# Value columns of all heads projected in the first head, element products in the ring of the level tiles, and a group's value products issued behind its last masked copy

## The chip, the core and the metric

The kernel runs on one core of one Trainium2 chip. A core has a matrix engine (TensorE, PE in the profile; its weight loads are listed as PEld), a vector engine (VectorE, DVE), a scalar engine (ScalarE, ACT), GpSimd (POOL) and an engine that mostly issues transfers (SyncE, SP). Each engine works through its own queue in order and waits on semaphores for the others. Data lies in SBUF (128 partitions); TensorE writes to PSUM, which has eight banks of 512 float32 columns for each partition. The metric is the device time of one launch in microseconds (us); the median of several runs is compared.

## What is computed

One decoder layer for 2048 positions of width 1024. The part that matters here is the mixing stage: a normalised input is projected to queries, forget gates, values and output gates of four HGRN2 heads, and to queries, keys and values of a sliding-window attention with eight query heads, two key heads and a sink logit in the softmax.

```python
u = rmsnorm(h, norm_mix_w[l])
proj = u @ w_in[l]
hq, hf, hi, hg, att = jnp.split(proj, [...], axis=-1)
f = lb + (1.0 - lb) * jax.nn.sigmoid(hf)
o_hg = hgrn2_chunkwise(q_hg, k_hg, v_hg, log_f)     # v_hg is hi, 4 heads of 128 columns
o_hg = rmsnorm(o_hg, hg_norm_w[l]) * silu(hg)
o_att = sliding_window_attention_with_sinks(aq, ak, av, sinks[l])
h = h + jnp.concatenate([o_hg, o_att], axis=-1) @ w_out[l]
```

The recurrence of a head is `S_t = diag(f_t) S_{t-1} + k_t v_t^T`, `o_t = S_t^T q_t`, with `k_t = 1 - f_t`. After the mixing stage come a gated feed-forward stage with a short convolution and a final normalisation.

## The kernel before

The sequence is worked in two halves of 1024 positions (`HALF`). In each, the mixing stage runs over four heads `h`; with each head goes one pair of attention query heads `j = h`. Then come the output projection (`out_proj`), the feed-forward stage (`gate_up`, `down`), and in the tail of `down` the first units of the next half.

A dense product in float32 is made of three matmuls on parts: weights and input are each split into a rounded part (`hi`, `xh`) and a rest (`lo`, `xl`), and hi·xh, hi·xl and lo·xh are summed in PSUM. `prep` loads 1024 columns of weights (SP issues the load into a ring of three, tag `raw`), ACT makes the rounded copy (L192) and DVE the rest (L193). Both go to a ring of two (tags `hi` and `lo`), or, with `slots`, to the ring of eight tiles with tag `m` in the pool `hp`, which also holds input tiles, the heads' queries and attention outputs. `unit` (L214) then makes 48 matmuls of 512 columns for 128 output rows.

For one head, `hgrn` is a generator that is driven in pieces:

- the units `f` and `hq` and their evictions;
- the levels: first two element products of the two halves of the columns, then seven levels with block sizes 1 to 64. `summed_products` multiplies on DVE (L546), splits the product (ACT L547, DVE L548) and sums it over the partitions with two matmuls (L550, L551, tile `pdiag`); it is called twice for the diagonal and once for the first level. For each of the other levels ACT copies a rearranged part of `QK` into a tile `G` (L598), four matmuls make `plev` (L609; L604 at block size 32), and DVE multiplies `QK` in place (L612) for the next level. Tile `QK` and tile `f` have one buffer each;
- transposes of K (L646), state updates (L653 on TensorE, L657 on DVE);
- the gate unit `g`, the output products (L671, L672), a norm and a transpose (L687).

`attend` makes the unit `q`, then scores and softmax for two groups of four query blocks, and then, for each group: four transposes for each key head (L497, tile `ppt`), and two masked copies of each on DVE (L500, tiles `po` and `pp`: the block's own keys and those of the block before). From these, 16 value products (L508, tile `poT`, 64 output rows each; float32, two instructions each on TensorE) sum the two key blocks for four query blocks and two key heads. ACT copies the result out (L512; in the last pair L518, whose result the output projection reads).

Values of the recurrent heads come from `project_v`, called in heads 0 and 2, each time for two heads: eight tiles of 128 positions, each with 24 matmuls of 256 columns (L706 to L708, tile `pvv`), evicted by two scaled copies on ACT (L710). Its matmuls stand behind the levels in the program, and TensorE works on them while the levels' small matmuls wait for ACT and DVE. In heads 1 and 3 no projection stands there; head 3 has its gate unit ahead of the levels and the first units of the output projection (L214, tile `pop`) behind them.

The program's order is not the queues' order. A planner simulates the engines and puts instructions into each queue by program order and by when it expects their inputs; `tc.issue_after(x)` keeps what is traced inside it behind `x` on the same engine, without a semaphore. The buffers of a tag are given out as they come free, and a tile whose ring is full makes its first writer wait.

Of the kernel before, what the change touches and what calls it, by code (L numbers as in the profile page):

```python
# [8 lines left out]
F32 = mybir.dt.float32  # L9
F32R = mybir.dt.float32r  # L10
U32 = mybir.dt.uint32
I32 = mybir.dt.int32
AF = mybir.ActivationFunctionType
# [26 lines left out]
NEG = -1.0e30  # L40
UT = 7
RAW = 3
VB = 2
GB = 2
WARM = 12
TAIL_WARM = 7
LV = 4
# [3 lines left out]
def hymba_layer(ctx: ExitStack, tc: tile.TileContext, a: dict, out: bass.AP):  # L51
# [380 lines left out]
    def attend(hf, j, X, invb, KS, V, mix, p):  # L432

        o = unit(a["w_att"][j], X, "q")
        qT = slot(f"att{j}")
        for b, bs in halves():
            nc.vector.scalar_tensor_tensor(qT[:, bs], o[b], 0.125, invb[:, bs], op0=ALU.mult, op1=ALU.mult)
            nc.scalar.activation(qT[:, bs], qT[:, bs], AF.Identity, bias=C.bq[:, j:j + 1])
        yield
        scs = []  # L440
        for g in range(NB):
            sc = p.tile([P, 2, 4, P], F32, tag="sc", name="sc", bufs=2)
            gs = slice(g * 512, (g + 1) * 512)
            for kv in range(2):
                r, other = rows(kv), rows(1 - kv)

                qh, ql = [p.tile([P, 512], F32R, tag="pp", name=n, bufs=4) for n in ("qh", "ql")]
                nc.scalar.copy(qh[r], qT[r, gs])
                nc.scalar.copy(qh[other], qT[r, gs])
                nc.vector.tensor_tensor(ql[r], qT[r, gs], qh[r].bitcast(F32), op=ALU.subtract)  # L450
                nc.scalar.copy(ql[other], ql[r].bitcast(F32))
                for i0 in (0, 2):
                    pb = ps("at", "psc")
                    first = hf == 0 and g == 0 and i0 == 0
                    for i in range(2):
                        n = g * 4 + i0 + i
                        w0 = 1 if first and i == 0 else 0
                        o = pb[:, i * 256 + w0 * P:(i + 1) * 256]
                        ks = slice((n + w0) * P, (n + 2) * P)
                        for t, qx in enumerate((qh, ql)):  # L460
                            nc.tensor.matmul(o, qx[:, (i0 + i) * P:(i0 + i + 1) * P], KS[:, kv, ks],
                                             start=t == 0, stop=t == 1)
                    pv = pb.rearrange("p (i w k) -> p i w k", i=2, w=2)
                    dst = sc[:, kv, i0:i0 + 2]
                    if first:
                        nc.vector.memset(dst[:, 0], NEG)
                        nc.scalar.copy(dst[:, 1], pv[:, 1, 0])
                    else:
                        nc.scalar.copy(dst, pv[:, :, 0])
                    nc.vector.copy_predicated(  # L470
                        dst, C.own.bitcast(U32).unsqueeze(1).to_broadcast([P, 2, P]), pv[:, :, 1])
            m = p.tile([P, 2, 4], F32, tag="mx", name="m", bufs=2)
            nc.vector.tensor_reduce(m.rearrange("p a b -> p (a b)"),
                                    sc.rearrange("p a b c -> p (a b) c"), axis=AX.X, op=ALU.max)
            sk = C.sinkb[:, j].unsqueeze(2).to_broadcast([P, 2, 4])
            nc.vector.tensor_tensor(m, m, sk, op=ALU.max)
            es = p.tile([P, 2, 4], F32, tag="es", name="es", bufs=2)
            nc.vector.tensor_tensor(es, sk, m, op=ALU.subtract)
            nc.vector.tensor_scalar(m, m, -1.0, None, op0=ALU.mult)
            den = p.tile([P, 2, 4], F32, tag="den", name="den", bufs=2)  # L480
            for kv in range(2):
                for i in range(4):
                    nc.scalar.activation(sc[:, kv, i], sc[:, kv, i], AF.Exp, bias=m[:, kv, i:i + 1],
                                         accum_out=den[:, kv, i:i + 1])
            nc.scalar.activation(es, es, AF.Exp)
            nc.vector.tensor_tensor(den, den, es, op=ALU.add)
            nc.vector.reciprocal(den, den)
            nc.vector.tensor_tensor(sc, sc, den.unsqueeze(3).to_broadcast([P, 2, 4, P]), op=ALU.mult)
            scs.append(sc)
        yield  # L490
        for g, sc in enumerate(scs):
            pm = []
            for kv in range(2):
                pm.append([p.tile([P, 4, P], F32, tag="pp", name=n, bufs=4) for n in ("po", "pp")])
                pt = ps("at", "ppt")
                for i in range(4):
                    nc.tensor.transpose(pt[:, i * P:(i + 1) * P], sc[:, kv, i], ident)  # L497
                ptv = pt.rearrange("p (i q) -> p i q", i=4)
                for dst, mk in zip(pm[kv], (C.ownT, C.prevT)):
                    nc.vector.tensor_tensor(dst, ptv, mk.unsqueeze(1).to_broadcast([P, 4, P]), op=ALU.mult)  # L500
            oT = ps("at", "poT")
            for i in range(4):
                n = g * 4 + i
                noprev = hf == 0 and n == 0
                for prev in range(1 if noprev else 2):
                    for kv in range(2):
                        r = rows(kv)
                        nc.tensor.matmul(oT[r, i * P:(i + 1) * P], V[:, n + 1 - prev, r], pm[kv][prev][:, i],  # L508
                                         start=prev == 0, stop=noprev or prev == 1)
            gs = slice(g * 512, (g + 1) * 512)  # L510
            if j < ATT_J - 1:
                nc.scalar.copy(qT[:, gs], oT)  # L512
                mix[4 + j] = qT
            else:
                if g == 0:
                    mix[4 + j] = new_x()
                h, l = mix[4 + j]
                nc.scalar.copy(h[:, gs], oT)  # L518
                nc.vector.tensor_tensor(l[:, gs], oT, h[:, gs].bitcast(F32), op=ALU.subtract)
            yield  # L520

    def hgrn(hf, h, X, invb, vs, WG, mix, p, fu=None):
# [18 lines left out]
        ST = p.tile([P, TT, P], F32, tag="t4", name="ST", bufs=2)  # L541
        def summed_products(x, y):

            d = p.tile([P, 512], F32, tag="dd", name="dd", bufs=2)
            hi, lo = [p.tile([P, 512], F32R, tag="dg", name=n, bufs=4) for n in ("dh", "dl")]
            nc.vector.tensor_tensor(d, x, y, op=ALU.mult)  # L546
            nc.scalar.copy(hi, d)  # L547
            nc.vector.tensor_tensor(lo, d, hi.bitcast(F32), op=ALU.subtract)  # L548
            o = ps("hg", "pdiag")
            nc.tensor.matmul(o, ones_r, hi, start=True, stop=False)  # L550
            marks[1] = nc.tensor.matmul(o, ones_r, lo, start=False, stop=True)  # L551
            return o
# [142 lines left out]

    def project_v(hf, parts, X, rs, p):

        v = [p.tile([P, TT, P], F32, tag="v", name="v", bufs=VB) for _ in range(2)]
        for tt in range(TT):
            o = ps("mm", "pvv")  # L700
            t = slice(tt * P, (tt + 1) * P)
            for kt in range(KT):
                hi, lo = parts[kt // 4]
                xh, xl = X[kt]
                c = slice((kt % 4) * 256, (kt % 4 + 1) * 256)
                nc.tensor.matmul(o[:, 0:256], xh[:, t], hi[:, c], start=kt == 0, stop=False)  # L706
                nc.tensor.matmul(o[:, 0:256], xl[:, t], hi[:, c], start=False, stop=False)
                nc.tensor.matmul(o[:, 0:256], xh[:, t], lo[:, c], start=False, stop=kt == KT - 1)  # L708
            for i in range(2):
                nc.scalar.activation(v[i][:, tt], o[:, i * P:(i + 1) * P], AF.Identity, scale=rs[:, tt:tt + 1])  # L710
        return v

    def split_into(h, l, src, eng=None):
        return (nc.scalar.copy(h, src),  # L714
# [480 lines left out]
    for hf in range(NH):  # L1195
        X, kv, invb, rs, f0 = nxt
        with ExitStack() as st:
# [5 lines left out]
            for h in range(HG):  # L1203
# [4 lines left out]
                if h == HG - 1:  # L1208
                    next(at)
                    next(hg)  # L1210
                    for kt in (0, 4, 1, 5, 2, 6):
                        M[kt] = split(mix[kt])
                    next(hg)
                elif h % 2 == 0:
                    next(at)
                    wv = [prep(a["w_v"][h // 2, s]) for s in range(2)]
                    next(hg)
                    vs += project_v(hf, wv, X, rs, p)
                else:
                    next(hg)  # L1220
                    next(at)
# [21 lines left out]
def _layout(i):  # L1243
# [14 lines left out]
    rows = [ar(P) + h * P for h in range(4)]  # L1258
    rows += [512 + np.concatenate([j * HD + ar(HD), (j + 4) * HD + ar(HD)]) for j in range(4)]
    w_out = i["w_out"][0][np.concatenate(rows)]  # L1260
    w_v = np.stack([cols(w_in, 1024 + pr * 256 + ar(256)).reshape(P, 2, D).transpose(1, 0, 2) for pr in range(2)])
    conv = np.concatenate([i["conv_w"][0], i["conv_b"]], 0)
    d = {
        "xT": x.T.reshape(KT, P, S),
# [37 lines left out]
```

## Time and profile before

| what | value |
|---|---|
| median of three runs | 2175.64 us |
| lowest and highest | 2173.93 and 2177.19 us |
| the profiled execution's own time | 2174.83 us |
| its span, first to last instruction | 2173.1 us |
| granted TensorE clock | 0.999 |
| moved by DMA | 258.09 MB, mean 119 GB/s |

The profile is one execution. Busy shares and durations are those of single instructions; matmuls overlap, so their distance in time, not their duration, is what they cost. Rows of groups give the line, the engine, the operation, the tiles (output, then inputs), the shape and the count, then the busy time, the mean duration in nanoseconds, and the idle time of that engine just before them with what ended it. Rows of the timeline give the start and the duration in us. Rows of windows give a stretch, its length, and the busy time of TensorE, weight loads, DVE, ACT and POOL in it, each with its number of instructions, then the granted clock, the DMA share and GB/s.

### The profile page before, as it was taken

The numbers are of one execution on the slowest core, as the hardware profiler recorded it, in microseconds if no ns is written. First come the engines' busy times: TensorE is split into PE (matmuls) and PEld (weight loads), VectorE is DVE, ScalarE is ACT, GpSimd is POOL, SyncE is SP. The second block draws the span as 40 slices with busy tenths as digits, with TensorE's granted clock in tenths as the row PEclk, the third lists the DMA queues.
The fourth block names the chain that finished last, engine by engine and source line by source line (L and its number), as shares of the span: only waits on it lengthen the run. The fifth ranks groups of instructions, "written<-read, shape, count | busy, mean of one in ns | idle before, by whom it ended". The sixth has DMA issues, their size and how long they took to land.

```text
span 2173.1 us, 29038 instructions
## 1 busy us (share of the span) xinstructions
PE 2151.3 (99%) x11136; PEld 1809.6 (83%) x11136; DVE 1659.9 (76%) x2446; ACT 1094.1 (50%) x1902; POOL 6.0 (0%) x28
## 2 busy tenths in 40 slices
PE   9999999999999999999999999999999999999998
PEld 7988987888888888788889889878888888888888
DVE  6677677688887878785866776777978888887766
ACT  6556556564444445335736466555544443444353
POOL 1000000000000000000000000000000000000000
PEclk9999999999999999999999999999999999999999
DMA  4101112413232235964631111124133323259643
GB/s 156 49 30 39 49 40 78 136 59 127 92 126 89 96 117 167 375 223 163 205 127 39 42 37 49 47 70 147 58 116 102 117 82 126 93 190 396 226 142 131
DMA packets 94387, 258.09 MB, mean 119 GB/s; under 512 B 11416, under 2 KB 17576, under 8 KB 94248
## 3 DMA queue, kind: packets, MB, share of 16 engines
q1 hardware_dynamic: 88992, 251.30, 34.2%
q10 hardware_dynamic: 5256, 4.94, 0.8%
q8 instruction: 87, 1.43, 0.3%
q14 instruction: 52, 0.43, 0.1%
HBM read 195.10 MB, written 57.15 MB: 116 GB/s over the span
## 4 chain that ended last, share of the span: by engine, by line
PE 93%; DVE 3%; ACT 2%; DMA 1%; issue 1%; SPq 0%; ACTq 0%; DVEq 0%
PE X L885 7%; PE pop L214 7%; PE X L887 7%; PE X L886 7%; PE hq L214 4%; PE f L214 4%; PE q L214 4%; PE g L214 4%; PE Y L885 4%; PE Y L886 4%; PE Y L887 4%; PE pdx L1098 3%; PE pdx L1096 3%; PE pdx L1097 3%; PE pdy L1096 3%; PE pdy L1097 3%
## 5 line engine op out<-in xcount | busy, mean ns | idle before, releaser
L714 ACT CAST whi<-raw 128x1024 fp32r<-128x1024 f32 x88 | 92.6, 1052 | 109.1 <-PE X L886 68.2
L885 PE MATMUL X<-T,whi 128*128 128x512 f32 x352 | 136.9, 389 | 0.0
L886 PE MATMUL X<-T,whi 128*128 128x512 f32 x352 | 136.9, 389 | 0.0
L887 PE MATMUL X<-T,wlo 128*128 128x512 f32 x352 | 136.9, 389 | 0.0
L980 DVE SCALAR_TENSOR_TENSOR y<-ga,cw,y 128x1024 f32<-128x1024 f32 x88 | 112.4, 1280 | 26.0 <-ACT y L978 26.0
L892 ACT COPY u<-X 128x512 f32<-128x512 f32 x88 | 51.5, 585 | 133.2 <-PE X L887 133.0
L715 DVE TENSOR_TENSOR wlo<-raw,whi 128x1024 fp32r<-128x1024 f32 x88 | 107.2, 1219 | 0.0
L715 DVE TENSOR_TENSOR xld<-raw,xhd 128x1024 fp32r<-128x1024 f32 x72 | 80.9, 1132 | 21.7 <-ACT xhd L714 21.2
L192 ACT CAST whi<-raw 128x1024 fp32r<-128x1024 f32 x57 | 59.9, 1050 | 72.2 <-PE pop L214 28.6
L714 ACT CAST xhd<-raw 128x1024 fp32r<-128x1024 f32 x72 | 69.6, 977 | 47.3 <-DMA raw<-act1T 15.5
L193 DVE TENSOR_TENSOR wlo<-raw,whi 128x1024 fp32r<-128x1024 f32 x57 | 69.2, 1217 | 26.4 <-ACT whi L192 26.3
L214 PE MATMUL pop<-XH,wlo 128*128 128x512 f32 x256 | 85.9, 390 | 0.0
L214 PE MATMUL pop<-XL,whi 128*128 128x512 f32 x256 | 85.2, 390 | 0.0
L214 PE MATMUL pop<-XH,whi 128*128 128x512 f32 x256 | 85.0, 393 | 0.0
L886 PEld LDWEIGHTS X<-T,whi 128*128 128x128 f32 x352 | 66.1, 188 | 13.8
L885 PEld LDWEIGHTS X<-T,whi 128*128 128x128 f32 x352 | 66.1, 188 | 13.7
L887 PEld LDWEIGHTS X<-T,wlo 128*128 128x128 f32 x352 | 66.1, 188 | 13.7
L1096 PE MATMUL pdx<-xhd,hid 128*128 128x512 f32 x192 | 74.5, 392 | 1.9 <-ACT hid L714 1.0
L1097 PE MATMUL pdx<-xld,hid 128*128 128x512 f32 x192 | 74.8, 390 | 0.0
L612 DVE TENSOR_TENSOR QK<-QK,f 128x1024 f32<-128x1024 f32 x56 | 68.5, 1223 | 8.2 <-ACT G L598 7.6
L1098 PE MATMUL pdx<-xhd,lod 128*128 128x512 f32 x192 | 73.7, 389 | 0.0
L706 PE MATMUL pvv<-whi,XH 128*128 128x256 f32 x256 | 72.7, 286 | 0.0
(384 smaller groups left out, 6601.1 us busy)
## 6 DMA issues: line engine op xcount, KB each, us to landing
wr<-in_w_down SPq DMA_DIRECT2D x90, 512.0 KB, 5.5
raw<-in_w_gate SPq DMA_DIRECT2D x44, 512.0 KB, 3.7
raw<-in_w_up SPq DMA_DIRECT2D x44, 512.0 KB, 3.7
raw<-act0T SPq DMA_DIRECT2D x20, 512.0 KB, 3.9
raw<-act1T SPq DMA_DIRECT2D x20, 512.0 KB, 5.7
act0B<-y SPq DMA_DIRECT2D x33, 256.0 KB, 2.2
act1B<-y SPq DMA_DIRECT2D x33, 256.0 KB, 2.8
raw<-in_w_out SPq DMA_DIRECT2D x16, 512.0 KB, 6.2
```

Source lines behind the costliest of these rows:

```text
L193: nc.vector.tensor_tensor(lo, raw, hi.bitcast(F32), op=ALU.subtract)
L214: marks["unit"] = nc.tensor.matmul(o[b], w, x[:, bs], start=f, stop=l)
L706: nc.tensor.matmul(o[:, 0:256], xh[:, t], hi[:, c], start=kt == 0, stop=False)
L714: return (nc.scalar.copy(h, src), (eng or nc.vector).tensor_tensor(l, src, h.bitcast(F32), op=ALU.subtract))
L715: (eng or nc.vector).tensor_tensor(l, src, h.bitcast(F32), op=ALU.subtract))
L885: nc.tensor.matmul(o, wh[:, ws], xh, start=i == 0 and not more, stop=False, skip_group_check=more)
L886: nc.tensor.matmul(o, wh[:, ws], xl, start=False, stop=False, skip_group_check=more)
L887: r = nc.tensor.matmul(o, wl[:, ws], xh, start=False, stop=i == 3, skip_group_check=more)
L980: nc.vector.scalar_tensor_tensor(y, g[:, w:w + HALF], C.cw[:, ft, w:w + 1], y, op0=ALU.mult, op1=ALU.add)
L1096: nc.tensor.matmul(o, wh[:, i, c], ah[:, i, cols], start=f, stop=False, skip_group_check=more)
L1097: nc.tensor.matmul(o, wh[:, i, c], al[:, i, cols], start=False, stop=False, skip_group_check=more)
L1098: nc.tensor.matmul(o, wl[:, i, c], ah[:, i, cols], start=False, stop=l, skip_group_check=more)
```

## The change

Four edits. The v tile holds all four heads and is made in head 0 in one projection: eight tiles of 128 positions with 24 matmuls of 512 columns, one copy out of PSUM for each, and four sets of prepared weights, two of them in the ring of eight; the weights' layout in memory follows. The tiles of `summed_products` move from tags of their own to the tag `G`, one for the product and one for both its parts, and that ring gets three buffers instead of two. In `attend` the value products of a group run from the last query block to the first, the block before ahead of the own block and the second key head ahead of the first, and all of them are kept behind the first one, which reads the group's last masked copy. The constant of the two v buffers goes.

```diff
-VB = 2
-GB = 2
+GB = 3
...
             oT = ps("at", "poT")
-            for i in range(4):
+            first = None
+            for i in (3, 2, 1, 0):
                 n = g * 4 + i
                 noprev = hf == 0 and n == 0
-                for prev in range(1 if noprev else 2):
-                    for kv in range(2):
+                for prev in (0,) if noprev else (1, 0):
+                    for kv in (1, 0):
                         r = rows(kv)
-                        nc.tensor.matmul(oT[r, i * P:(i + 1) * P], V[:, n + 1 - prev, r], pm[kv][prev][:, i],
-                                         start=prev == 0, stop=noprev or prev == 1)
+                        with tc.issue_after(first) if first else ExitStack():
+                            mm = nc.tensor.matmul(oT[r, i * P:(i + 1) * P], V[:, n + 1 - prev, r], pm[kv][prev][:, i],
+                                                  start=noprev or prev == 1, stop=prev == 0)
+                        first = first or mm.ins
...
         def summed_products(x, y):
 
-            d = p.tile([P, 512], F32, tag="dd", name="dd", bufs=2)
-            hi, lo = [p.tile([P, 512], F32R, tag="dg", name=n, bufs=4) for n in ("dh", "dl")]
+            d = p.tile([P, 2, 512], F32, tag="G", name="dd", bufs=GB)[:, 0]
+            both = p.tile([P, 2, 512], F32R, tag="G", name="dh", bufs=GB)
+            hi, lo = both[:, 0], both[:, 1]
...
-        v = [p.tile([P, TT, P], F32, tag="v", name="v", bufs=VB) for _ in range(2)]
+        v = p.tile([P, HG, TT, P], F32, name="v")
...
-                hi, lo = parts[kt // 4]
+                hi, lo = parts[kt // 2]
                 xh, xl = X[kt]
-                c = slice((kt % 4) * 256, (kt % 4 + 1) * 256)
-                nc.tensor.matmul(o[:, 0:256], xh[:, t], hi[:, c], start=kt == 0, stop=False)
-                nc.tensor.matmul(o[:, 0:256], xl[:, t], hi[:, c], start=False, stop=False)
-                nc.tensor.matmul(o[:, 0:256], xh[:, t], lo[:, c], start=False, stop=kt == KT - 1)
-            for i in range(2):
-                nc.scalar.activation(v[i][:, tt], o[:, i * P:(i + 1) * P], AF.Identity, scale=rs[:, tt:tt + 1])
-        return v
+                c = slice((kt % 2) * 512, (kt % 2 + 1) * 512)
+                nc.tensor.matmul(o, xh[:, t], hi[:, c], start=kt == 0, stop=False)
+                nc.tensor.matmul(o, xl[:, t], hi[:, c], start=False, stop=False)
+                nc.tensor.matmul(o, xh[:, t], lo[:, c], start=False, stop=kt == KT - 1)
+            nc.scalar.activation(v[:, :, tt], o.rearrange("p (h d) -> p h d", h=HG), AF.Identity,
+                                 scale=rs[:, tt:tt + 1])
+        return [v[:, h] for h in range(HG)]
...
-                elif h % 2 == 0:
+                elif h == 0:
                     next(at)
-                    wv = [prep(a["w_v"][h // 2, s]) for s in range(2)]
+                    wv = [prep(a["w_v"][s], s > 1) for s in range(4)]
                     next(hg)
                     vs += project_v(hf, wv, X, rs, p)
...
-    w_v = np.stack([cols(w_in, 1024 + pr * 256 + ar(256)).reshape(P, 2, D).transpose(1, 0, 2) for pr in range(2)])
+    w_v = cols(w_in, 1024 + ar(512)).reshape(P, 4, D).transpose(1, 0, 2)
```

## Prediction

> **What bounds the kernel now.** I read the page first: its span, the busy shares and the chain that ended last.
>
> ```profile
> span 2173.1 us, 29038 instructions
> ...
> PE 2151.3 (99%) x11136; PEld 1809.6 (83%) x11136; DVE 1659.9 (76%) x2446; ACT 1094.1 (50%) x1902; POOL 6.0 (0%) x28
> ...
> PE 93%; DVE 3%; ACT 2%; DMA 1%; issue 1%; SPq 0%; ACTq 0%; DVEq 0%
> ```
>
> TensorE is busy all the time and 93% of the last chain is its own; DVE has 76%, ACT half. Two things can therefore shorten the run: fewer nanoseconds on TensorE's stream, or less of the small rest in which it waits. Two things can lengthen it: DVE falling behind, or a wait that TensorE's queue did not have. A matmul's busy time overlaps that of its neighbours, so I price TensorE by the distance between starts. The second view is that of the windows, in the first half's mixing stage (DVE is the third pair of numbers, ACT the fourth).
>
> ```profile
> 178.00:227.00 49.00, 49.00 (x332) 41.15 (x331) 38.97 (x82) 28.91 (x82) 0.00 (x0) 1.00 0.12 36
> 227.00:257.50 30.50, 30.50 (x281) 30.07 (x280) 18.72 (x30) 18.25 (x38) 0.00 (x0) 1.00 0.12 34
> ...
> 338.00:375.00 37.00, 33.32 (x277) 28.78 (x275) 28.71 (x70) 21.45 (x75) 0.00 (x0) 1.00 0.17 56
> ```
>
> 227 to 257.5 is head 2 with the second value projection: TensorE full, DVE 61%. In 178 to 227, which has no projection, DVE is at 80% and TensorE is still full. Only 338 to 375, the end of the stage, shows it waiting: 3.7 us.
>
> **The projection.** Third view: the groups by line, then starts in the timeline, then the chain.
>
> ```profile
> L706 PE MATMUL pvv<-whi,XH 128*128 128x256 f32 x256 | 72.7, 286 | 0.0
> ...
> L193 DVE TENSOR_TENSOR wlo<-raw,whi 128x1024 fp32r<-128x1024 f32 x57 | 69.2, 1217 | 26.4 <-ACT whi L192 26.3
> ...
> L192 ACT CAST whi<-raw 128x1024 fp32r<-128x1024 f32 x57 | 59.9, 1050 | 72.2 <-PE pop L214 28.6 <-PE hq L214 13.6 <-PE q L214 8.4
> ...
> L892 ACT COPY u<-X 128x512 f32<-128x512 f32 x88 | 51.5, 585 | 133.2 <-PE X L887 133.0
> ...
> L710 ACT ACTIVATE v<-pvv,y 128x128 f32<-128x128 f32 x64 | 20.1, 362 | 12.4 <-PE pvv L708 12.4
> ...
> L547 ACT CAST dh<-dd 128x512 fp32r<-128x512 f32 x24 | 14.9, 621 | 27.3 <-DVE dd L546 21.7 <-PE pdiag L550 5.6
> ```
> ```profile
> 77.02 0.28 PE L707 MATMUL pvv<-whi,XL 128*128 128x256 f32 x1
> ...
> 79.89 0.28 PE L707 MATMUL pvv<-whi,XL 128*128 128x256 f32 x1
> ```
> ```profile
> 380.14 65.52 PE pop L214 x289
> ```
>
> From 77.02 to 79.89 lie 24 matmuls of 256 columns: 2.87 / 24 = 119.6 ns each. The chain's 289 matmuls of 512 columns take 65.52 us: 226.7 ns each, with one weight load each as well. So 256 columns cost more than half of 512: 2 x 119.6 - 226.7 = 12.5 ns of every pair is a fixed part. Before: 3 x 256 = 768 matmuls (L707 and L708 go with L706 step by step), 768 x 119.6 ns = 91.9 us. After: 384 of 512 columns, 384 x 226.7 ns = 87.1 us. **Term 1: -4.8 us**, all of it on the path.
>
> The Trainium skill, "TensorE: Matmul & The Clock Gate", section "Back-to-back issue gap", gives a warm gap of N/2.4 + 2.5 ns. By that rule the merging would save 2.5 ns for each of 384 pairs, an estimate of 1.0 us; the trace does not agree, its fixed part is 12.5 ns, and the sum goes by the trace.
>
> ACT evicts 16 tiles of 512 columns instead of 64 of 128. At the price of L892, 16 x 0.585 = 9 us replace 64 x 0.362 = 23 us; but ACT waits for TensorE there (12.4 us), so this is worth nothing on the path. Prepared weights stay eight sets of 1024 columns, but sets two and three of a half move from head 2 to head 0, into the ring of eight of `hp`. SP issues their loads ahead of those of w_g and the next w_f:
>
> ```profile
> raw<-in_w_v SPq DMA_DIRECT2D x8, 512.0 KB, 3.9
> ```
>
> Two loads of 3.9 us and two casts (L192) with their subtractions (L193) lie under the first two units of head 0 and a projection that now has 192 x 226.7 ns = 43.5 us of matmuls. I cost it at nothing; were that cover gone (the ring of eight still held by x tiles), it is one load, cast and subtraction, 3.9 + 1.05 + 1.22 = 6.2 us once in a half. POOL has nothing in this stage. The v tiles of all heads stand from head 0, so no head waits for a v buffer.
>
> **The value products.** One group has 16 products, 32 instructions of TensorE. Twelve groups end in L512, four (the last attention pair) in L518:
>
> ```profile
> L512 ACT COPY att<-poT x12: 585/586/588, 133.1 to 1384.0; 128x512 f32<-128x512 f32 x12
> L518 ACT CAST XH<-poT x4: 562/574/589, 368.0 to 1453.5; 128x512 fp32r<-128x512 f32 x4
> ```
> ```profile
> 138.57 0.48 PE L214 MATMUL hq<-XH,wlo 128*128 128x512 f32 x1
> 138.98 0.43 PE L508 MATMUL poT<-po,V 128*64 128x128 f32 x2
> 139.34 0.74 PE L214 MATMUL hq<-XH,whi 128*128 128x512 f32 x2
> ...
> 144.05 0.39 PE L214 MATMUL hq<-XL,whi 128*128 128x512 f32 x1
> 144.37 0.32 PE L508 MATMUL poT<-po,V 128*64 128x128 f32 x1
> ...
> 146.26 0.50 PE L214 MATMUL hq<-XL,whi 128*128 128x512 f32 x1
> ```
>
> The first product of a group runs alone, as soon as its own mask is there: 0.36 us for two instructions (138.98 to 139.34). The other 30 follow 5 us later in 1.89 us (144.37 to 146.26), 63 ns each, since the two half-width products of a pair overlap. Entering such a group costs 144.37 - 144.05 - 0.227 = 0.09 us over the usual distance. All twelve are cut this way, from the first to the last:
>
> ```profile
> 130.23 0.43 PE L508 MATMUL poT<-po,V 128*64 128x128 f32 x2
> ```
> ```profile
> 1376.58 0.43 PE L508 MATMUL poT<-po,V 128*64 128x128 f32 x2
> ```
>
> With every product issued behind one that reads the last mask, the first can't go ahead. It saves 0.36 + 0.09 and lengthens the rest by 0.12: 0.33 us in each of 12. **Term 2: -4.0 us.**
>
> The four groups at the end of the two stages lose. There the queue has nothing else:
>
> ```profile
> 363.45 0.40 PE L508 MATMUL poT<-po,V 128*64 128x128 f32 x2 [1.52 <-DVE pp L500]
> ...
> 364.07 0.68 DVE L500 TENSOR_TENSOR pp<-ppt,prevT 128x512 f32<-128x512 f32 x1
> 364.22 0.54 PE L508 MATMUL poT<-po,V 128*64 128x128 f32 x5 [0.36 <-DVE po L500]
> ...
> 366.05 0.49 PE L671 MATMUL po<-v,ST 128*128 128x128 f32 x2
> ```
> ```profile
> 372.26 0.40 PE L508 MATMUL poT<-po,V 128*64 128x128 f32 x2
> ...
> 373.44 0.32 PE L508 MATMUL poT<-pp,V 128*64 128x128 f32 x1 [0.16 <-DVE pp L500]
> ...
> 375.11 0.50 PE L214 MATMUL pop<-XH,whi 128*128 128x512 f32 x1
> ```
>
> The last mask of the first one ends at 364.75. Before, part of the group was done by then. After, all of it (2.0 us) follows: it ends at 366.8 instead of 366.05. The second has its last mask at 373.4 and would end at 375.45 instead of 375.11. Queued behind the waiting product are the other 15, then L671 and the out-projection (L214, pop), for which L518 makes the operand. That is 0.7 + 0.35 us, up to 2.1 us in both stages; at the first group L671 needs DVE's running sums anyway, so I take **term 3: +1.5 us** (0 to 2.1).
>
> **The ring of three.** d takes one slot of G, hi and lo another, so the third product of a head still waits for TensorE to finish the first, as ACT does now (L547 waits 5.6 us for pdiag on the whole run). The copies G (L598) may wait for one subtraction of 512 columns more (0.7 us, as L500's product) in a head, with other casts queued behind them on ACT. TensorE has whole units as cover; 0, at most 8 x 0.7 = 5.5 us.
>
> **Moving 23 us of TensorE work out of head 2.** This is the open term. Head 2 loses its projection as cover for the seven levels, and head 0 gets cover that it doesn't need. The trace shows head 1 without one. Its levels begin 6.4 us after its q unit begins; those of head 2 begin 7.6 us after theirs:
>
> ```profile
> 148.59 6.81 PE q L214 x30
> ```
> ```profile
> 155.01 1.22 DVE L612 TENSOR_TENSOR QK<-QK,f 128x1024 f32<-128x1024 f32 x1
> ```
> ```profile
> 213.23 0.62 PE L214 MATMUL q<-XH,whi 128*128 128x512 f32 x2
> ...
> 220.84 1.22 DVE L612 TENSOR_TENSOR QK<-QK,f 128x1024 f32<-128x1024 f32 x1
> ```
>
> So head 2 finds TensorE's queue almost as head 1 found it, and head 1 passed without a gap: one round of the chain took 220.84 - 155.01 = 65.8 us, and heads 1 and 2 need (160 - 23) / 2 = 68.5 us of TensorE each (118 to 278, less the projection). A second such round should pass too; the second half runs the same program and counts the same. **Term 4: 0**, between -7.4 us and +18.5 us, whose ends are the rivals below. Sum: 2174.8 - 4.8 - 4.0 + 1.5 = 2167.5 us on the profiled execution's own time (2174.83, 0.8 under the median of the three runs); beside the median, 2168.3 us.
>
> **Rivals.** *DVE becomes the bound in heads 1 to 3: slower.*
>
> ```profile
> 178.00:278.00 100.00, 100.00 (x742) 89.76 (x741) 71.00 (x140) 62.17 (x161) 0.00 (x0) 1.00 0.13 39
> ...
> 118.00:375.00 257.00, 253.32 (x1680) 217.75 (x1679) 191.83 (x364) 149.42 (x374) 0.00 (x0) 1.00 0.17 50
> 600.00:700.00 100.00, 100.00 (x443) 82.81 (x442) 80.58 (x105) 40.99 (x62) 0.00 (x0) 1.00 0.34 114
> ```
>
> 178 to 278 would have 77 us for 71.0 - 2.4 = 68.6 us of DVE: 89%. The most I see with TensorE full is 80% (38.97 of 49; 80.58 of 100). Held to 79.5%, DVE needs 86.3 us, 9.3 more in each half: 2167.5 + 18.5 = 2186.0, beside the median 2187. It decides where DVE's work can't be put off past head 2. Against it: over 118 to 375 DVE would need 189.4 of 234 us, 81%, just what the feed-forward stage shows. *In between:* even so 189.4 / 0.795 = 238.2 us, 4.2 too many in a half: 2176, beside the median 2177.
> *The end of the stage gains:* work put off from head 2 fills the 3.7 us in which TensorE waits before the out-projection; 2 x 3.7 less: 2160, beside the median 2161. Against it, that end hangs on DVE and ACT, and they get the work put off too.
> *The change doesn't do what it says:* the planner cuts groups elsewhere, or the order changes leave as many entries; without term 2, 2171.5, beside the median 2172.
> *The fixed part is not saved:* the 12.5 ns belong to something that 512-column matmuls with these weights meet as well, and a pair still costs 239 ns; term 1 is gone, 2172.3, beside the median 2173. The 512-column row, measured with a load for each matmul, speaks against it. The Trainium skill's rule above ("Back-to-back issue gap") would lead near it.
>
> **How the numbers follow.** 0.2% (4.35 us), about what a measurement of this kernel can tell from no change, puts the borders at 2171.3 and 2180.0. Forecast 2168: 0.42 (0.38 faster, 0.04 same). In between: 0.18 (0.13 same, 0.05 slower). DVE bound: 0.14, slower. End gains: 0.12, faster. Change not as said: 0.10 (0.02 faster, 0.08 same). Fixed part: 0.04, same. Faster 0.52, same 0.29, slower 0.19. The range goes from 2159 (the gain at the end, less the forecast's own spread) to 2183: it leaves out most of the DVE-bound case and little else. The forecast's own range is 2165 to 2171.
>
> **What would show it.** Right: pvv starts 227 ns apart in head 0 alone; no group of L508 cut in two; TensorE's stretch from head 1 to the out-projection 23 us shorter with no new gap. Wrong: waits of L653, L508 or a unit of L214 for DVE or ACT that grow between heads 2 and 3, DVE's share there staying at 80% while TensorE idles; or an idle time before the out-projection well over 5 us.

## The result and the profile after

The changed kernel takes 2167.36 us (median of 6 runs, 2166.65 to 2168.53) against 2175.47 us for the kernel before (6 runs beside it): a ratio of 0.9964 [0.9954, 0.9975], 8.1 us less. A second set gave 0.9970 [0.9959, 0.9982]. The forecast was 2168.3, in the range 2159 to 2183. Two terms of its sum failed, in opposite directions; the experiments show that.

The page of the kernel after, its lines for the span, the busy shares and the last chain:

```profile
span 2164.9 us, 28224 instructions
...
PE 2142.5 (99%) x10752; PEld 1790.8 (83%) x10752; DVE 1658.0 (77%) x2446; ACT 1091.6 (50%) x1858; POOL 6.5 (0%) x28
...
PE 93%; DVE 4%; ACT 1%; DMA 1%; issue 1%; SPq 0%; ACTq 0%; DVEq 0%
```

TensorE is as full as before and still carries 93% of the chain. It has 384 matmuls less (11136 - 10752). The windows of the kernel after, in the first half, from head 1 to the out-projection (columns as in the prediction: DVE is the third pair; the last row is the whole stretch, which begins with head 1's unit f):

```profile
195.00:260.50 65.50, 65.50 (x429) 56.12 (x429) 51.30 (x103) 41.26 (x102) 0.00 (x0) 1.00 0.12 37
260.50:312.60 52.10, 52.10 (x363) 45.02 (x363) 43.63 (x91) 31.45 (x88) 0.00 (x0) 1.00 0.14 41
312.60:369.00 56.40, 52.88 (x377) 45.72 (x375) 50.98 (x96) 43.08 (x103) 0.00 (x0) 1.00 0.27 84
139.80:369.00 229.20, 225.68 (x1478) 193.04 (x1477) 187.62 (x361) 144.17 (x355) 0.00 (x0) 1.00 0.16 51
```

Without the projection in head 2, DVE reaches 51.30 / 65.50 = 78%, then 84%, then 90%, and TensorE has no gap until 312.60. The rival that held DVE to 79.5% fell by this row alone: 84% and a full TensorE stand side by side. The list of TensorE's waits of the kernel after (in total, times, longest) has small ones only; its first three rows:

```profile
PE plev L612 <- ACT G L601: 2.0, 2, 1.3
PE plev L612 <- DVE ST L586: 1.8, 1, 1.8
PE ppt L496 <- DVE sc L469: 1.8, 1, 1.8
```

So the 8 us are hardly waits that went: the span less TensorE's busy time is 2173.1 - 2151.3 = 21.8 us before and 2164.9 - 2142.5 = 22.4 us after. They come from the stream. But where in it, the one comparison can't say: three edits changed it at once.

### The profile page after: what moved, and what is told of

It is laid out like the page before. It is cut to its first block, busy times and chain, and to the rows that moved or that the text cites. A ratio compares the mean times of both kernels' runs of the same rounds, so it can differ in the third digit from the quotient of the medians.

```text
span 2164.9 us, 28224 instructions
## 1 busy us (share of the span) xinstructions
PE 2142.5 (99%) x10752; PEld 1790.8 (83%) x10752; DVE 1658.0 (77%) x2446; ACT 1091.6 (50%) x1858; POOL 6.5 (0%) x28
## 3 DMA queue, kind: packets, MB, share of 16 engines
q8 instruction: 84, 1.38, 0.3%
## 4 chain that ended last, share of the span: by engine, by line
PE 93%; DVE 4%; ACT 1%; DMA 1%; issue 1%; SPq 0%; ACTq 0%; DVEq 0%
PE X L888 7%; PE X L889 7%; PE X L890 7%; PE pop L213 7%; PE hq L213 4%; PE f L213 4%; PE q L213 4%; PE Y L890 4%; PE Y L888 4%; PE Y L889 4%; PE g L213 4%; PE pdx L1099 3%; PE pdx L1101 3%; PE pdx L1100 3%; PE pdy L1101 2%; PE pdy L1100 2%
## 5 line engine op out<-in xcount | busy, mean ns | idle before, releaser
L888 PE MATMUL X<-T,Sh 128*128 128x512 f32 x176 | 68.7, 390 | 1.5 <-ACT s L895 1.5
```

The source lines that it names most:

```text
L888: nc.tensor.matmul(o, wh[:, ws], xh, start=i == 0 and not more, stop=False, skip_group_check=more)
```

## Experiments

Each run lists its mean granted clock. What a run lost to a lower clock is its time x (1 - clock); the time less that is called "at full clock" below. The clock is given to three decimals, so one run is known to 1.1 us and only means are used. This reading came after the runs; the expectations did not have it. It takes off too much: within the sets, over 182 runs, a run's time rises by 0.60 +- 0.05 us for each us of this loss (about two thirds, if the rounding of the clock is allowed for). Some of the low clock falls where TensorE has nothing to do: from 2160 to 2165 us the kernel after shows a clock of 0.88 and no matmul. With two thirds of the loss taken off, ring_alone would be 7.3 us over before instead of 6.0, the change 8.0 us under it instead of 8.8, and all_but_projection 1.6 us over instead of 0.3 under; no other sign in the table turns. Means in us, with the difference from the kernel before of the same set and its standard error:

```
kernel              runs  mean     lost to clock  at full clock  less before
before (three sets)   74  2174.2   3.2 to 4.1     2170.4-2170.8
values_alone          11  2170.2   5.5            2164.7          -5.8 +- 0.4
ring_alone             5  2183.9   7.4            2176.4          +6.0 +- 0.9
all_but_projection    11  2179.4   8.9            2170.5          -0.3 +- 0.4
all_but_values        11  2170.7   3.4            2167.3          -3.1 +- 0.4
narrow_in_head0       11  2174.9   8.3            2166.6          -3.8 +- 0.6
halved                11  2175.0   7.3            2167.7          -3.1 +- 0.6
ring_five             11  2172.9   2.2            2170.7          -0.1 +- 0.4
one_slot              11  2170.6   7.1            2163.5          -7.3 +- 0.6
last_pair_eager        9  2168.8   6.5            2162.3          -8.6 +- 0.8
after (first set)      6  2167.5  5.4            2162.1
changed_again          6  2168.5   6.5            2162.0          -8.8 +- 0.9
one_slot_half2         5  2164.2   4.8            2159.5         -11.3 +- 0.7
```

### The value products alone

The kernel before with only the hunk in `attend`.

> The new order of the value products alone, on the kernel before (2175.5 us). Theory (TensorE's stream sets the time, each edit is priced by its own starts): twelve groups are no longer cut, 12 x 0.33 to 0.44 us less, and the four groups at the ends of the stages lose up to 1.5 us together: 2171.5 to 2173. Rival 1 (the ends of the stages set the time, the cut groups lay in slack): no gain or a loss, 2175.5 to 2177. Rival 2 (the lone first product filled a gap): groups stay cut or new gaps appear before L508, 2175.

Measured: 2169.95 us against 2173.81, 0.9982 [0.9974, 0.9991], 3.9 us less; the theory gave 2.5 to 4. All twelve groups run whole: TensorE's timeline has the value products in 16 stretches, where the kernel before has them in 28. (In the kernel after, two of the twelve have state updates between their products, from 290.78 and from 1360.94 on.) A whole group in the timeline of the kernel after:

```profile
164.94 0.61 PE L213 MATMUL hq<-XL,whi 128*128 128x512 f32 x2
165.48 0.44 PE L509 MATMUL poT<-pp,V 128*64 128x128 f32 x4
...
167.38 0.73 PE L213 MATMUL hq<-XH,wlo 128*128 128x512 f32 x2
167.95 0.62 PE L213 MATMUL q<-XH,whi 128*128 128x512 f32 x2
```

The whole group, 32 instructions, takes 167.38 - 165.48 = 1.90 us. Before, 30 of them took 1.89 and the two of the lone product 0.36 more, with 0.09 for entering once more. A group saves 0.36 + 0.09 - 0.01 = 0.44 us, twelve of them 5.3. This sum leaves out that leaving a group costs something too: the two matmuls from 167.38 to 167.95 take 0.57 us, 0.12 over twice 0.227. Where a group stands among matmuls of 512 columns, the saving is thus about 0.56 us; not all twelve do. At full clock the run shows 5.8 +- 0.4, less what the longer waits at the stage's end (below) took from it.

What it gave back is a wait of the kind of term 3, with a second cost that no step of the prediction had. Of values_alone, at the first group of the last pair: DVE's last masked copy, TensorE's timeline, and the windows:

```profile
362.36 0.68 DVE L500 TENSOR_TENSOR pp<-ppt,prevT 128x512 f32<-128x512 f32 x1
```
```profile
359.18 1.04 PE L497 MATMUL ppt<-ident,sc 128*128 128x128 f32 x8
363.18 0.70 PE L510 MATMUL poT<-pp,V 128*64 128x128 f32 x4 [2.96 <-DVE m L479]
363.63 0.67 PE L510 MATMUL poT<-po,V 128*64 128x128 f32 x4
...
366.26 0.49 PE L674 MATMUL po<-v,ST 128*128 128x128 f32 x2
```
```profile
363.18:364.40 1.22, 1.22 (x12) 1.22 (x14) 1.11 (x4) 1.22 (x7) 0.00 (x0) 0.50 0.00 0
```

TensorE waits 2.96 us for the last mask, which ends at 362.36 + 0.68 = 363.04 (the row names L479, the short operation that DVE does right behind it), and the group then needs 366.26 - 363.18 = 3.08 us instead of 1.90: four instructions lie 0.45 us apart, not 0.22. The third number from the right says why: the granted clock is 0.50.

### The ring alone

The kernel before with only the hunks of `summed_products` and `GB = 3`.

> Element products in the level tiles' ring of three alone, on the kernel before (2175.5 us). Theory (TensorE has whole units as cover): within 1 us, 2174.5 to 2176.5. Rival 1 (the third product and the copies G wait for a slot and the chain of levels gets longer): up to 0.7 us in each of 8 heads, 2176.5 to 2181. Rival 2 (three slots for the levels let the copies run ahead and the ends of the stages gain): 2170 to 2174.

Measured: 2183.72 against 2173.81, 1.0042 [1.0028, 1.0055], 9.1 us **more**. TensorE's waits of ring_alone name the place, at the start of the transposes of K in head 3, once in each half:

```profile
PE pkn L647 <- ACT ST L637: 7.6, 2, 3.9
```

How a ring costs that is read from ACT's timeline. The first two copies G of head 3 in the kernel before, then the same stretch in ring_alone:

```profile
315.77 1.19 ACT L598 COPY G<-QK 128x1024 f32<-128x1024 f32 x1 [2.44 <-DVE QK L612]
...
319.56 1.05 ACT L598 COPY G<-QK 128x1024 f32<-128x1024 f32 x1
```
```profile
319.49 0.62 ACT L548 CAST dh<-dd 128x512 fp32r<-128x512 f32 x1
...
320.63 1.21 ACT L599 COPY G<-QK 128x1024 f32<-128x1024 f32 x1
...
327.92 1.05 ACT L599 COPY G<-QK 128x1024 f32<-128x1024 f32 x1
```

Before, the products had tiles of their own, and the first copy came at 315.77, ahead of the third product's cast. Now the three slots are held by the parts of the first two products and by the third product, until TensorE has summed the first; its sums stand behind a whole unit, at 318.80 and 319.04 in TensorE's timeline of ring_alone:

```profile
318.80 0.40 PE L551 MATMUL pdiag<-dh,ones_r 128*128 128x512 f32 x1
```

Only then comes the third product's cast (319.49), and the first level's copy behind it: 4.9 us later than before, and the second level's copy 8.4 us. While TensorE has whole units to do, this costs nothing. It costs at the stage's end. ACT's timeline there, ring_alone first, the kernel before second:

```profile
355.18 0.74 ACT L633 COPY ST<-plev 32x256 f32<-32x256 f32 x2 [2.64 <-DVE ST L587]
355.93 1.28 ACT L485 ACT_TABLE_LOAD   x1
...
360.54 0.75 ACT L637 COPY ST<-plev 64x256 f32<-64x256 f32 x2
```
```profile
352.82 0.37 ACT L636 COPY ST<-plev 64x256 f32<-64x256 f32 x1
353.21 1.28 ACT L485 ACT_TABLE_LOAD   x1
```

Before, the last level's copies ran just ahead of the softmax (table load and eight exponentials). Late, they stand behind all of it, 355.93 to 360.54. TensorE in ring_alone, and its clock in the windows:

```profile
361.34 1.11 PE L647 MATMUL pkn<-ident,QK 128*128 128x128 f32 x4 [3.93 <-ACT ST L637]
362.50 3.78 PE L654 MATMUL pu<-v,Kn 128*128 128x128 f32 x16
```
```profile
355.90:359.40 3.50, 1.50 (x14) 1.26 (x12) 0.00 (x0) 3.47 (x14) 0.00 (x0) 1.00 0.00 0
359.66:363.07 3.41, 1.68 (x6) 1.29 (x7) 2.42 (x6) 3.31 (x11) 0.00 (x0) 0.50 0.00 0
363.07:366.48 3.41, 3.41 (x18) 3.41 (x17) 1.81 (x4) 0.00 (x1) 0.00 (x0) 0.50 0.02 5
```

During the wait the clock goes to half, for 2 x 3.41 us, and the 16 state updates take 3.78 us. The same updates in TensorE's timeline of the kernel before:

```profile
359.01 2.05 PE L653 MATMUL pu<-v,Kn 128*128 128x128 f32 x16 [1.36 <-ACT Kn L647]
```

So the ring costs +6.0 +- 0.9 us at full clock and 7.4 - 3.5 = 3.9 us through the clock. Both the theory and Rival 1 had it too small.

### Everything but the value products, and the projection narrow

`all_but_values` is the change without its hunk in `attend`. `narrow_in_head0` is the change with the whole projection in head 0, but in 256 columns:

```diff
+VB = 4
...
-                    wv = [prep(a["w_v"][s], s > 1) for s in range(4)]
+                    wv = [prep(a["w_v"][s // 2, s % 2], s > 1) for s in range(4)]
                     next(hg)
-                    vs += project_v(hf, wv, X, rs, p)
+                    for s in (0, 2):
+                        vs += project_v(hf, wv[s:s + 2], X, rs, p)
```

> The change without the new order of the value products: one projection of 512 columns in head 0 and the ring of three. Theory (fixed part of 12.5 ns for each of 384 pairs saved, cover moved at no cost): 4.8 us less than before, 2170 to 2171.5. Rival 1 (DVE falls behind in head 2 without the projection as cover and gives the gain back): 2174 to 2185, with new waits of TensorE in heads 2 and 3. Rival 2 (moving the work out of head 2 gains by itself at the ends of the stages): 2165 to 2168.

> The change, but with two projections of 256 columns one behind the other in head 0 (four v tiles, 768 matmuls as before). It moves the cover and saves no fixed part. Theory (the fixed part of 12.5 ns is saved by width): 4.8 us more than the changed kernel's 2167.4, 2171 to 2173.5, pvv starts 120 ns apart. Rival (the gain is that of moving the work to head 0): 2166.5 to 2169.

Measured: 0.9985 [0.9976, 0.9993] (2170.41) and 1.0003 [0.9994, 1.0012] (2174.62, against 2173.81 both). The first, 3.4 us less, is 1.4 us short of its theory and fits neither rival. The second lies 1.0003 - 0.9964 = 0.0039 of before, 8.5 us, behind the change (7.2 by the second set), and not the 4.8 that its theory gave; a part of that is clock (8.3 us lost against 5.4 and 6.5). At full clock narrow_in_head0 lies 8.8 - 3.8 = 5.0 +- 1.1 us behind the change (changed_again).

### The ring and the value products, without the projection

Both hunks on the kernel before.

> The change without the projection in head 0 (two projections of 256 columns in heads 0 and 2 as before): ring of three and new order of the value products on the kernel before. Measured so far: ring alone 1.0042, value products alone 0.9982 of before. Theory (the edits add up, and the ring is the loss that the projection in head 0 pays for): 1.0042 x 0.9982 = 1.0024, about 5 us over before. Rival (the ring's loss is an accident of one planned order): 0.997 to 1.000, it does not return here.

Measured: 2179.08 against 2173.68, 1.0024 [1.0015, 1.0032]; the product of the two single ratios is 1.0042 x 0.9982 = 1.0024. The two parts add, and the ring's wait is still there in the list of waits:

```profile
PE pkn L650 <- ACT ST L640: 7.7, 2, 3.9
```

From here to narrow_in_head0 only the place of the projection differs, with the v buffers and the slots of prepared weights that it needs. That is -3.8 + 0.3 = -3.5 +- 0.7 us at full clock, and the lists of waits of narrow_in_head0 and of the kernel after have no such row. ACT's timeline of the kernel after, where the last level's copies come right behind those of the level before, with no softmax between:

```profile
353.93 0.74 ACT L635 COPY ST<-plev 32x256 f32<-32x256 f32 x2 [1.62 <-DVE ST L589]
354.69 0.75 ACT L639 COPY ST<-plev 64x256 f32<-64x256 f32 x2
```

### The ring with five slots

ring_alone with one number changed.

```diff
-GB = 3
+GB = 5
```

> Ring alone, but with five slots instead of three (without the four-head v tile there is room), on the kernel before. Theory (the ring costs because three products hold up to two slots each until their sums run on TensorE behind the gate unit of head 3, so the copies G wait for a slot): the loss of ring alone goes, 0.999 to 1.001 of before, the first copies G of head 3 start before the gate unit ends. Rival (the loss has nothing to do with slots, the planner's order merely fell badly): 1.003 to 1.005 again.

Measured: 2173.05 against 2173.68, 0.9995 [0.9986, 1.0003]. The wait at L647 is gone and the first copy is back, in ACT's timeline of ring_five:

```profile
315.88 1.20 ACT L599 COPY G<-QK 128x1024 f32<-128x1024 f32 x1 [1.12 <-DVE QK L613]
```

So it is the number of slots that costs, not the shared tag or the one tile for both parts. Five slots in the changed kernel were not tried.

### The product in another ring, and the last pair in the old order

`one_slot` is the changed kernel with d in the ring of the masked copies; `last_pair_eager` gives the last pair's four groups the old order without `issue_after`.

```diff
-            d = p.tile([P, 2, 512], F32, tag="G", name="dd", bufs=GB)[:, 0]
+            d = p.tile([P, 512], F32, tag="pp", name="dd", bufs=4)
```
```diff
-            first = None
-            for i in (3, 2, 1, 0):
+            first, late = None, j < ATT_J - 1
+            for i in (3, 2, 1, 0) if late else range(4):
...
-                        with tc.issue_after(first) if first else ExitStack():
+                        with tc.issue_after(first) if first and late else ExitStack():
```

> The changed kernel, with the product d in the ring of four of the attention's masked copies (tag pp) instead of a slot of G; its two parts stay in one slot of G. Theory (slots of G are short at the end of the stage, here too): part of the ring's loss comes back, 2160 to 2166 where the changed kernel has 2167.4 (0.993 to 0.996 of before). Rival 1 (the changed kernel no longer hangs on the ring, its levels run early enough): the same within 1 us, 0.996 to 0.997. Rival 2 (d now waits for masked copies): slower, 0.997 to 1.000.

> The changed kernel, but the four groups of the last attention pair keep the old order and start with their first mask. Theory (these four lose up to 2.1 us together when they wait for the last mask): 0.5 to 2 us less than the changed kernel, 0.9955 to 0.9962 of before. Rival (the idle time before the output projection only moves): the same, 0.9960 to 0.9968.

Measured: one_slot 2170.06, 0.9982 [0.9974, 0.9991]; last_pair_eager 2168.79, 0.9974 [0.9964, 0.9984]; both against 2173.68. Freeing a slot in both halves brings no gain (-7.3 against -8.8 at full clock); the ratio lies where Rival 2 put it. The changed kernel's waits for G (2.0 us, both in the second half) are gone in one_slot's list, but others stand there that the changed kernel doesn't have: 3.6 us for Kn, 3.4 for masked copies, 3.0 ahead of the scores. That d waits for masked copies, Rival 2's reason, is not shown. The old order in the last pair brings no gain that these runs can tell: -8.6 +- 0.8 against -8.8 +- 0.9 at full clock, and the ratio is above both expectations. TensorE's timeline of the kernel after has one reason:

```profile
356.10 2.05 PE L656 MATMUL pu<-v,Kn 128*128 128x128 f32 x16
358.08 0.44 PE L509 MATMUL poT<-pp,V 128*64 128x128 f32 x4
...
367.24 0.44 PE L509 MATMUL poT<-pp,V 128*64 128x128 f32 x4 [1.38 <-DVE y L171]
```

The first tail group finds its last mask done (DVE ends it at 357.40) and starts without a wait, where values_alone waited 2.96 us. The second still waits 1.38 us until its last mask is done (367.09). The waits for a mask of the kind in values_alone are also in the list of all_but_projection (4.7 us in two) and not in that of narrow_in_head0: they went with the move of the projection.

### The change again, its width halved, and a joined version

`halved` keeps everything of the change, the order of the program and the single copy included, but makes each matmul of the projection as two of 256 columns into the same bank:

```diff
-            for kt in range(KT):
...
-                c = slice((kt % 2) * 512, (kt % 2 + 1) * 512)
-                nc.tensor.matmul(o, xh[:, t], hi[:, c], start=kt == 0, stop=False)
+            for half in (0, 256):
+                oc = o[:, half:half + 256]
+                for kt in range(KT):
...
+                    c = slice((kt % 2) * 512 + half, (kt % 2) * 512 + half + 256)
+                    nc.tensor.matmul(oc, xh[:, t], hi[:, c], start=kt == 0, stop=False)
```

`one_slot_half2` puts d in the other ring in the second half only:

```diff
+            d = (p.tile([P, 512], F32, tag="pp", name="dd", bufs=4) if hf else
+                 p.tile([P, 2, 512], F32, tag="G", name="dd", bufs=GB)[:, 0])
```

> The changed kernel once more, unedited, as the measure for the other two of this set. Expected: 0.9955 to 0.9975 of before, as measured first (0.9964).

> The changed kernel, with each matmul of 512 value columns made as two of 256 (first all steps of the left half, then all of the right), into the same bank, with the same weights and the same single eviction: the width alone. Theory (a fixed part of 12.5 ns a pair): 384 x 12.5 ns = 4.8 us over the changed kernel, its ratio plus 0.0022, pvv starts 120 ns apart. Rival 1 (the width is worth more, 8 to 9 us, as the difference to the two narrow projections suggests): plus 0.004. Rival 2 (the slack at the ends of the stages takes it up): plus 0 to 0.0005.

> The changed kernel, with the product d in the masked copies' ring in the second half of the sequence alone. In the traces the changed kernel's first half is the shortest (start to the last out-projection product 439.3 us) and the one_slot kernel's second half is (435.8 us from there on to the same point, against 440.2). Theory (each half's end is set by its own planned order, and the two can be joined): 3 to 4 us under the changed kernel, 2162 to 2165, ratio 0.9945 to 0.9955. Rival (the second half's order depends on the state that the first leaves, and falls otherwise): the same as the changed kernel or worse.

Measured against 2174.62: changed_again 2168.16, 0.9970 [0.9959, 0.9982]; halved 2174.49, 0.9999 [0.9990, 1.0008]; one_slot_half2 2164.51, 0.9950 [0.9938, 0.9962].

The stretch itself shows the width. The projection of the first half in TensorE's timeline, first and last start and what follows, of the kernel after and of halved:

```profile
69.05 0.39 PE L709 MATMUL pvv<-whi,XH 128*128 128x512 f32 x1
...
118.43 0.22 PE L460 MATMUL psc<-KS,qh 128*128 128x128 f32 x1
```
```profile
69.09 0.28 PE L711 MATMUL pvv<-whi,XH 128*128 128x256 f32 x1
...
120.84 0.22 PE L460 MATMUL psc<-KS,qh 128*128 128x128 f32 x1
```

49.38 us against 51.75: 2.37 us for 192 pairs, 12.3 ns each, and 4.7 us for both halves. At full clock the runs differ by 5.7 +- 1.1 us; by the ratios it is 0.0029, which alone does not tell the theory's 0.0022 from Rival 1's 0.004. Each matmul has a weight load of its own in both kernels, so halving the width also doubles the loads, and the fixed part may belong to either; no run separates them.

one_slot_half2 beats both kernels. Its reason was one_slot's trace, which looked better in the second half only. That reason doesn't hold in full. These rows give the first and the last of the casts of the attention result for the out-projection, of the kernel after and of one_slot:

```profile
L520 ACT CAST XH<-poT x4: 569/586/587, 361.3 to 1443.0; 128x512 fp32r<-128x512 f32 x4
```
```profile
L520 ACT CAST XH<-poT x4: 557/574/587, 369.5 to 1447.8; 128x512 fp32r<-128x512 f32 x4
```

From the first to the last, one_slot seems 1081.7 - 1078.3 = 3.4 us shorter. But in the kernel after two stretches at half clock lie in between, 3.4 us together (their rows stand in the last section), and none of one_slot's does (its own, 6.8 us long, comes before the first cast): at full clock the two are alike there. What remains of the joined version at full clock is 2162.0 - 2159.5 = 2.5 +- 1.1 us. The waits for G, 2.0 us in the kernel after, are gone in its list, and one of 2.9 us ahead of the scores is new; which instructions give the gain is open.

## Why the prediction came out right

- **What bounds the kernel:** right. TensorE's stream, then waits at the stage's end. Missing was that the clock goes to half behind waits there (values_alone, ring_alone, the kernel after).
- **Term 1, the width, -4.8:** right in mechanism and size: 4.7 us on the stretch. The rival in which the fixed part is not saved fell, and so did the 2.5 ns of the Trainium skill ("TensorE: Matmul & The Clock Gate", section "Back-to-back issue gap"), which that section gives for the isolated gap: the pairs differ by 12.3 ns.
- **Term 2, -4.0, and term 3, +1.5:** the mechanism was right, the sizes were off. A group saves 0.44 us, not 0.33, because the whole group is hardly longer than the 30 instructions were, which makes 5.3 us; the 0.12 us for leaving a group were missing too. Together the sum had -2.5; alone they measured -3.9. Term 3's wait is real where the ring and the projection stand as before (values_alone, 2.96 us); in the changed kernel one of 1.38 us is left, and the old order in these four groups gained nothing that the runs can tell.
- **The ring, 0, at most 5.5: this step failed.** Alone it costs 9.1 us. The prediction named the wait for a slot and then said that TensorE has whole units as cover. It has, at that place; the delay travels down the seven levels to where there is no cover, falls behind the softmax on ACT, and costs 3.8 us of waiting in each half, with the clock at half behind it.
- **Moving 23 us out of head 2, 0: this step failed too.** It gave -3.5 +- 0.7 us at full clock. Head 2 passed without its cover, as forecast. But the price of the ring went with the move: the rows that waited 7.7 us are gone. So "the end of the stage gains" came in part, through a wait that the prediction had not seen arise.
- **The sum:** at full clock -5.8 (values), +6.0 (ring), -3.5 (move) and -4.7 (width, from the stretch) is -8.0; measured -8.8 +- 0.9. Through the clock some 2 us are given back (6.5 lost against 4.1). The forecast of -7.3 lies between the measured -8.1 and -6.5 because its misses nearly cancel: ring +6.0, values -5.8 against -2.5, move -3.5, width +0.1, clock +2.4, in sum +1.7. That they do so is luck; only the width came out by its own reasoning.
- **DVE as the bound:** fell, 84% beside a full TensorE.

Open: the move without the ring was not tried. The v tile of four heads takes 8 KB more of each partition than the two buffers of before, just what the shared ring frees. So whether the move gains by itself, or only repairs what the ring broke, is not separated. That the move took the ring's wait away is read from the rows that vanish. That 2.4 us more are lost to the clock has no cause shown beyond the waits at the stage's end.

## What to carry to other kernels

Price a smaller ring not where its slot is waited for, but by following the delay to the end of the stage, and look there for what on the same engine's queue it falls behind. Take out what the granted clock cost before splitting a few microseconds among edits: here between 2 and 9 us of a kernel's time went by it, more than most of these edits are worth, and it made one half of a stage look faster than it was. Where a matmul's fixed part shows in two rows of different width, merging widths brings just that.

## What the runs showed of the hardware

**The clock dropped after short waits.** The lower clock comes in stretches of about 3.41 us at 0.50 (359.66 to 363.07 in ring_alone), or of several such, so each costs at most 1.7 us. The windows of the kernel after, in the second half's end of the stage:

```profile
1419.60:1423.00 3.40, 1.30 (x10) 0.97 (x8) 3.33 (x7) 2.49 (x6) 0.00 (x0) 1.00 0.26 74
1423.00:1426.40 3.40, 3.01 (x40) 2.37 (x40) 3.40 (x7) 0.51 (x1) 0.00 (x0) 0.51 0.11 34
1426.40:1429.80 3.40, 1.54 (x13) 1.23 (x14) 3.40 (x10) 2.47 (x6) 0.00 (x0) 0.99 0.00 0
1429.80:1433.20 3.40, 3.40 (x34) 3.07 (x31) 1.29 (x3) 2.22 (x13) 0.00 (x0) 0.52 0.02 5
```

A window with TensorE busy for 1.30 of 3.40 us is followed by one at half clock, and so is one with 1.54; the longest single wait of TensorE in this run is 1.8 us (the list of waits above). In the first window it has two, 0.72 us and the most of 1.76. The Trainium skill ("TensorE: Matmul & The Clock Gate", section "What's actually happening") gives two states, half and full, and a free-running window of 3413 ns; the stretches agree with both. Its section "HAM oscillation — how this bites in real kernels" gives gaps over about 3.4 us as what to avoid; here no gap was longer than 1.8 us. In the kernel before the clock once dropped without any gap. TensorE's timeline there, and its windows:

```profile
1092.41 0.95 PE L268 MATMUL pst<-ones,sums 128*128 128x1 f32 x8
...
1093.78 1.84 PE L268 MATMUL pst<-ones,invb 128*128 128x1 f32 x16
```
```profile
1096.00:1099.50 3.50, 3.50 (x10) 2.74 (x9) 3.40 (x19) 1.04 (x1) 0.00 (x0) 0.55 0.22 77
```

Just ahead of it, 24 matmuls of one column fill most of 3 us. They alone do not bring the drop: the same 24 begin at 1086.13 in the kernel after and at 1085.89 in changed_again, which is the same program, and behind them the windows, first of the kernel after, then of changed_again, are

```profile
1087.50:1096.00 8.50, 8.50 (x47) 7.31 (x46) 6.24 (x27) 1.05 (x1) 0.00 (x0) 1.00 0.55 191
```
```profile
1088.20:1095.00 6.80, 6.80 (x22) 5.59 (x22) 5.35 (x24) 1.04 (x1) 0.00 (x0) 0.53 0.33 122
```

So one execution of the same instructions lost 3.2 us there and another nothing. What decides it, no run shows.

**A lone product of 64 rows costs more than its place in a row of them.** In the kernel before its two instructions take 0.36 us alone; 32 instructions together take 0.01 us more than 30. How much of the 0.36 us is the empty other half and how much the change between float32 and rounded matmuls, no run separates.
